# A hybrid attention block on one core: forgetting scores negated, mask and minimum in one instruction, 1/sum applied at the branch; the two halves of each head's output stored apart and added in DRAM

## The chip, the cores and the metric

The kernel runs on one core of a Trainium2 chip. The metric is the device time of one execution in microseconds. The engines are TensorE (PE, with its weight loads PEld), VectorE (DVE), ScalarE (ACT), GpSimd (POOL) and SyncE (SP); each has its own queue of instructions and works it off in order. DMAs are issued from the queues of SP and POOL.

## The reference, cut to what matters

One decoder block over 1024 positions of width 1024: three gated attention branches (8 stick-breaking heads of 64, 8 forgetting heads of 64, 4 heads of 128 over 256 memory tokens), merged, and a squared-ReLU MLP. All in float32. The change touches the two causal kinds of heads and, in two lines, the others.

```python
def stick_breaking_attention(q, k, v):
    ...
        z = einsum(q, k) * HD ** -0.5
        strict = s_idx < t_idx
        log_rem = where(strict, log_sigmoid(-z), 0.0)
        after = cumsum(log_rem, reverse=True) - log_rem
        w = where(strict, exp(log_sigmoid(z) + after), 0.0)
        outs.append(einsum(w, v))

def forgetting_attention(q, k, v, log_f):
    F = cumsum(log_f)
    ...
        z = einsum(q, k) * HD ** -0.5
        z = z + F[t] - F[s]
        p = softmax(where(s_idx <= t_idx, z, NEG_INF))
        outs.append(einsum(p, v))

def reference(...):
    h = rmsnorm(x)
    ... = split(h @ w_in)                       # q, k, v of all heads, forget logits, gate logits
    o_fox = forgetting_attention(rmsnorm(fx_q), rmsnorm(fx_k), fx_v, log_sigmoid(f_logit + b_forget))
    ...
    merged = gate0 * (o_sb @ w_branch_sb) + gate1 * (o_fox @ w_branch_fox) + gate2 * (o_mem @ w_branch_mem)
    x = x + merged @ w_out
    x = x + relu(rmsnorm(x) @ w_ff_up) ** 2 @ w_ff_down
```

## The kernel before, in words

**Numbers.** Each float32 operand of a product is split into a high and a low part that PE takes at its faster rate (`hi` and `lo`, or `h` and `l` in the tiles' names), and a product is made of three passes: hi·hi, hi·lo, lo·hi. ACT copies the high part (L1029 for weights, `whi`), DVE subtracts it from the whole (L1030, `wlo`).

**What sets the order.** The program does not issue instructions as it is read. Each piece of work is a generator that yields `Op(engine, cost, fn)`, takes buffers with `Get` from lists of free ones (`Places`) and gives them back with `put`, and waits for an `Event`. A planner plays all generators forward in time with costs by formula (`mm_time`, `act_time`, `dve_time`, `SMALL` for a 128x1 instruction) and emits each instruction when its turn comes. What comes out is one fixed order for each engine. The hardware then runs it, with semaphores between the engines. A cost changed in one place so moves instructions everywhere behind it, and an instruction that takes longer on the chip than the planner charged makes its engine late against that order.

**Stages.** To about 340 us: the norm, the projections of all heads, the turning of queries and keys. 340 to 850: attention. 830 to 1000: the three branch products, in the order memory, stick-breaking, forgetting (`bring`, L1550, gets a branch's operand). Then merge, output product and MLP. Between the instructions of attention, the planner places the products of the gates (L1119, weights loaded as `raw<-w_in` on POOL's queue at L1037), so that PE is always fed.

**Attention.** Heads go in pairs, first the four stick-breaking pairs, then the four forgetting ones. A pair loads its queries and keys (`h`, L979) and values (`v`, L1015) on POOL's queue. A unit (`unit`, L875) is one head with two query tiles of 128; a pair has eight units. A query tile's keys come in one or two chunks of up to 512 columns, each with a score bank `sc` in PSUM (two banks).

For a stick-breaking tile (`sb_tile`, L785): scores on PE (L795), on the diagonal a mask added (the tile `strict`), two sigmoids on ACT (L800), a running product on DVE (L814). For a forgetting tile (`fox_tile`, L823), chunk by chunk: scores on PE (L837, L838; the forgetting sums F ride along as four more rows of the queries and keys, from `fq_scr` and `fk_scr`), on the diagonal a mask added (L843, the tile `above`), the maximum (L844), its negative (L845), then the exponential on ACT with its row sum (L848). After both chunks: the joint maximum (L856), factors for the chunks, the reciprocal of the sum (L865, L867), and a scaled copy of the whole weight tile on ACT (L871).

Then the weights are turned on PE (L904) and split (ACT L909 `pth`, DVE L911 `ptl`), and multiplied with the values on PE (L921) into the one `pv` bank. The part from the high values stands in its rows 0 to 63 and that from the low ones in its rows 64 to 127; their sum is the output. ACT copies the one half to a tile `ob` (L939; there are three), DVE adds the other (L940), and SP stores the 64x256 result to `o_scr` (L942), from where the branch reads it (L1554).

**Tiles.** PSUM: three `pp`, two `sc`, two `tr`, one `pv`. SBUF: `h`, `v`, `e` (weight tiles), `r` (also lent elsewhere by the name RR), `raw`, `ob`. The mask `above` (128x129: zeros and, above the diagonal, -1e30) is made on POOL at the program's start.

## Time and profile before

| | before |
|---|---|
| median of three runs | 1706.46 us (1706.36 to 1706.93) |
| the profiled execution | 1706.93 us, of which the profile's span is 1705.1 |
| HBM read, written | 181.44 MB, 88.60 MB |
| PE clock granted | 1.00 |

The page of the profile gives busy times of engines over the span, the chain of waits that ended last, and groups of instructions by line. Names right of the arrow are what an instruction reads. A table by stretches has, for each stretch of time: its bounds, its length, the busy time (and number of instructions) of PE, PEld, DVE, ACT, POOL, the granted clock of PE, the mean share of DMA engines that are busy, and GB/s. A row of waits reads: engine, tile and line of the one that waits, then what it waits for, then the time in all, the number, and the longest. A row of a timeline: start, duration, engine, line, operation, tiles, and in brackets the wait ahead of it and who ended it. A row of a tile or a line: durations as shortest, median and longest in ns, and from when to when in the program.

### The profile page before, as it was taken

The numbers are of one execution on the slowest core, as the hardware profiler recorded it, in microseconds if no ns is written. First come the engines' busy times: TensorE is split into PE (matmuls) and PEld (weight loads), VectorE is DVE, ScalarE is ACT, GpSimd is POOL, SyncE is SP. The second block draws the span as 40 slices with busy tenths as digits, with TensorE's granted clock in tenths as the row PEclk, the third lists the DMA queues.
The fourth block names the chain that finished last, engine by engine and source line by source line (L and its number), as shares of the span: only waits on it lengthen the run. The fifth ranks groups of instructions, "written<-read, shape, count | busy, mean of one in ns | idle before, by whom it ended". The sixth has DMA issues, their size and how long they took to land.

```text
span 1705.1 us, 25350 instructions
## 1 busy us (share of the span) xinstructions
PE 1691.7 (99%) x9186; PEld 1442.8 (85%) x9186; DVE 1346.3 (79%) x2321; ACT 886.8 (52%) x1635; POOL 256.0 (15%) x441
## 2 busy tenths in 40 slices
PE   9999999999999999999999999999999999999998
PEld 9998899998888888888888887878888887888887
DVE  7977678868999888888656898987777776788775
ACT  6445555556676798889733446533233344332331
POOL 0000000043322233241000011021211120000000
PEclk9999999999999999999999999999999999999999
DMA  7545444576544453553375642144444484554532
GB/s 242 162 144 191 135 124 149 157 245 187 160 128 123 113 176 112 183 164 110 100 238 168 217 179 94 56 162 141 156 153 149 142 289 180 195 206 148 198 123 74
DMA packets 131406, 271.72 MB, mean 159 GB/s; under 512 B 15761, under 2 KB 43409, under 8 KB 131281
## 3 DMA queue, kind: packets, MB, share of 16 engines
q1 hardware_dynamic: 99600, 169.94, 29.2%
q0 software_dynamic: 31680, 100.17, 19.5%
q8 instruction: 72, 1.18, 0.3%
q14 instruction: 54, 0.43, 0.1%
HBM read 181.44 MB, written 88.60 MB: 158 GB/s over the span
## 4 chain that ended last, share of the span: by engine, by line
PE 83%; issue 7%; DVE 5%; DMA 2%; POOL 2%; ACT 1%; SPq 0%; POOLq 0%; DVEq 0%; ACTq 0%
PE pp L1119 21%; PE pp L2518 7%; PE pp L1405 7%; PE pp L1848 6%; PE sc L1405 5%; PE tr L904 4%; PE tr L2518 4%; PE sc L2518 4%; PE sc L1119 3%; PE sc L1848 3%; PE pv L2518 2%; PE pv L921 2%; PE pp L921 2%; PE pv L1405 2%; POOL s_scr L1865 2%
## 5 line engine op out<-in xcount | busy, mean ns | idle before, releaser
L1119 PE MATMUL pp<-hi,whi 128*128 128x512 f32 x368 | 147.6, 401 | 0.0
L1119 PE MATMUL pp<-hi,wlo 128*128 128x512 f32 x368 | 145.0, 394 | 0.0
L1119 PE MATMUL pp<-lo,whi 128*128 128x512 f32 x368 | 144.8, 393 | 0.0
L1030 DVE TENSOR_TENSOR wlo<-raw,whi 128x1024 fp32r<-128x1024 f32 (+1 forms) x82 | 100.0, 1221 | 38.9 <-ACT whi L1029 38.6
L2518 PE MATMUL pp<-h,sop 128*128 128x512 f32 x540 | 128.7, 395 | 1.4 <-DVE sop L1784 1.4
L2518 PEld LDWEIGHTS pp<-h,sop 128*128 128x128 f32 x540 | 101.1, 187 | 26.5 <-DVE sop L1784 1.8
L1848 PE MATMUL pp<-h,oh 128*128 128x512 f32 x384 | 120.9, 396 | 0.7 <-ACT cu L1934 0.6
L1029 ACT ACTIVATE whi<-raw 128x1024 fp32r<-128x1024 f32 (+1 forms) x82 | 86.8, 1059 | 52.4 <-PE pp L1405 18.7
L911 DVE TENSOR_TENSOR ptl<-tr,pth 128x512 fp32r<-128x512 f32 (+1 forms) x160 | 98.8, 627 | 11.0 <-ACT pth L909 10.6
L909 ACT ACTIVATE pth<-tr 128x512 fp32r<-128x512 f32 (+1 forms) x160 | 86.7, 558 | 28.5 <-PE tr L904 15.5
L814 DVE TENSOR_TENSOR_SCAN r<-r,sm 128x896 f32<-128x896 f32 (+4 forms) x64 | 85.5, 1345 | 3.5 <-ACT r L799 3.4
L2436 ACT ACTIVATE h<-t 128x2048 fp32r<-128x2048 f32 x16 | 30.7, 1919 | 110.4 <-DVE t L1784 97.9
L1848 PEld LDWEIGHTS pp<-h,oh 128*128 128x128 f32 x384 | 71.7, 187 | 19.2 <-ACT cu L1934 1.5
L1119 PEld LDWEIGHTS pp<-hi,wlo 128*128 128x128 f32 x368 | 69.1, 188 | 16.4
L1119 PEld LDWEIGHTS pp<-lo,whi 128*128 128x128 f32 x368 | 69.5, 189 | 10.3
L1119 PEld LDWEIGHTS pp<-hi,whi 128*128 128x128 f32 x368 | 69.4, 189 | 10.1
L1848 PE MATMUL pp<-h,ol 128*128 128x512 f32 x192 | 75.9, 396 | 0.0
L1841 ACT ACTIVATE oh<-raw 128x512 fp32r<-128x512 f32 x64 | 39.4, 625 | 61.7 <-DVE raw L1784 61.7
L2518 PE MATMUL sc<-h,sop 128*128 128x512 f32 x264 | 63.4, 395 | 0.0
L2518 PE MATMUL tr<-h,sop 128*128 128x512 f32 x264 | 63.4, 395 | 0.0
L1784 DVE TENSOR_TENSOR sop<-ur,sop 128x2048 fp32r<-128x2048 f32 x27 | 61.7, 2286 | 1.7 <-ACT sop L2447 1.7
L844 DVE TENSOR_REDUCE st<-sc 128x1 f32<-128x512 f32 (+2 forms) x96 | 53.3, 555 | 9.3 <-PE sc L838 7.1
(586 smaller groups left out, 5102.9 us busy)
## 6 DMA issues: line engine op xcount, KB each, us to landing
ur<-s_scr SPq DMA_DIRECT2D x26, 1024.0 KB
raw<-w_in POOLq DMA_DIRECT2D x42, 512.0 KB, 5.2
raw<-w_up SPq DMA_DIRECT2D x60, 256.0 KB
s_scr<-s POOLq DMA_DIRECT2D x60, 256.0 KB, 2.5
g<-w_down SPq DMA_DIRECT2D x14, 1024.0 KB
s_scr<-cu POOLq DMA_DIRECT2D x48, 256.0 KB, 2.9
gate_scr<-o SPq DMA_DIRECT2D x44, 256.0 KB
o<-gate_scr SPq DMA_DIRECT2D x32, 256.0 KB
```

The source lines that it names most:

```text
L814: nc.vector.tensor_tensor_scan(out=rev, data0=rev, data1=zero.to_broadcast([P, n]), initial=1.0, op0=ALU.mult, op1=ALU.add)
L904: nc.tensor.transpose(tr[:, jj * 256 + a * P:jj * 256 + (a + 1) * P], es[a][:, j * P:(j + 1) * P], ident)
L909: yield Op("ACT", act_time(512 - lo_c), lambda: nc.scalar.activation(ph[:, lo_c:], tr[:, lo_c:], AF.Copy))
L911: yield Op("DVE", dve_time(512 - lo_c), lambda: nc.vector.tensor_tensor(pl[:, lo_c:], tr[:, lo_c:], f32(ph[:, lo_c:]), ALU.subtract))
L921: nc.tensor.matmul(pv[0][:, c_:256], pair.v[:, j, b, :], p_[:, jj * 256 + c_:(jj + 1) * 256], start=(k == 0 and n_ == 0 and i == 0), stop= ...
L1029: yield Op("ACT", 0.03 + act_time(m), lambda: nc.scalar.activation(hi, raw, AF.Copy))
L1030: yield Op("DVE", dve_time(m), lambda: nc.vector.tensor_tensor(lo, raw, f32(hi), ALU.subtract))
L1119: nc.tensor.matmul(ps, a_, b_, start=(first and i == 0), stop=(last and i == n - 1))
L1405: nc.tensor.matmul(out_, a_, b_, start=(first and n == 0 and j == 0), stop=(last and n == 3 and j == len(todo) - 1), skip_group_check=True)
L1784: nc.vector.tensor_tensor(out_, a_, b_, op)
L1848: nc.tensor.matmul(ps, w[a_][:, k * P:(k + 1) * P], h[b_][k], start=(first and k == 0 and i == 0), stop=(last and k == 3 and i == 2), skip ...
L2518: nc.tensor.matmul(ps, a_[:, c, qs], b_[:, c, :], start=(kind in ("P1", "P2", "P7") and c == 0 and i == 0), stop=(kind in ("P2", "P4", "P3 ...
```

## The change

**Signs.** The forgetting queries' gain and the signs of the stored F are flipped, so that the bank holds the negated scores; the stick-breaking queries are negated as they are split. All masks then are +1e30 above the diagonal, in one tile `later` of 128x513, made on POOL when attention's tiles are opened, in place of `above`.

**A forgetting tile.** The chunk on the diagonal has one DVE instruction that adds the mask and gives the row's minimum (which is the negated maximum, as the exponential's bias needs it); the other chunk has a plain minimum. A second chunk waits for the first one's minimum and takes the joint one as its bias, the exponential having scale -1. With two chunks the first is then brought to the joint minimum by one product on DVE; with one chunk nothing more is done. The weights are not divided by their sum any more. The sums are kept in columns of a tile `fn`.

**1/sum.** When a pair is through, DVE takes the reciprocal of its 16 columns and SP stores them to `l_scr`, element by element (128x16x1). The forgetting branch loads them, spread over 64 partitions for each head, and multiplies its operand by them on DVE (128x1024) before the split.

**Output halves.** ACT copies all 128 rows of the `pv` bank to `ob`, which frees the bank; SP stores the two halves apart, to `o_scr` and to `low_scr`. After a pair's eighth unit, and a pause of 4 us in the plan, POOL issues a DMA that adds 128 rows of `low_scr` to `o_scr` in DRAM. The branch of the forgetting heads waits for the event `added` in place of `over`.

**Also.** In memory attention the maximum is taken with its negative in one instruction. The tiles for small statistics are fewer and smaller.

```diff
-    above = C.p.tile([P, P + 1], F32, tag="above", name="above")
-    nc.gpsimd.memset(above, 0.0)
-    nc.gpsimd.affine_select(out=above, in_=above, pattern=[[-1, P + 1]], compare_op=ALU.is_ge,
-                            fill=NEG, base=0, channel_multiplier=1)
...
+    low_scr = [dram.tile([512, S], F32, name=f"low_scr{b}", tag=f"low_scr{b}") for b in range(2)]
+    l_scr = dram.tile([8, S], F32, name="l_scr", tag="l_scr")
...
-            nc.vector.tensor_scalar(gq2, gq2, HD ** -0.5, None, ALU.mult)
+            nc.vector.tensor_scalar(gq2, gq2, -HD ** -0.5, None, ALU.mult)
...
+    def sums_kept(h0):
+
+        cols = fn[:, 8 * h0:8 * h0 + 16]
+        yield Op("DVE", SMALL, lambda: nc.vector.reciprocal(cols, cols))
+        yield Op("SP", 0.4, lambda: nc.sync.dma_start(
+            l_scr[h0:h0 + 2, :].rearrange("h (i p) -> p (h i)", p=P), cols, allow_slow_non_contiguous=True), 4.0)
...
-                nc.vector.tensor_reduce(mx, sc.rearrange("p (t m) -> p t m", m=MEM), AX.X, ALU.max)
-                nc.vector.tensor_scalar(mx, mx, -1.0, None, ALU.mult)
+                nc.vector.tensor_reduce(mx, sc.rearrange("p (t m) -> p t m", m=MEM), AX.X, ALU.max, negate=True)
...
             def maxima():
                 if c + u == n:
-                    dg = sc[:, u - P:u]
-                    nc.vector.tensor_tensor(dg, dg, tri, ALU.add)
-                nc.vector.tensor_reduce(mx[:, ci:ci + 1], sc[:, :u], AX.X, ALU.max)
-                nc.vector.tensor_scalar(nx[:, ci:ci + 1], mx[:, ci:ci + 1], -1.0, None, ALU.mult)
+                    nc.vector.tensor_tensor_reduce(sc[:, :u], sc[:, :u], holder["later"][:, 512 - u:512], 1.0, -NEG,
+                                                   ALU.add, ALU.min, nx[:, ci:ci + 1])
+                else:
+                    nc.vector.tensor_reduce(nx[:, ci:ci + 1], sc[:, :u], AX.X, ALU.min)
             yield Op("PE", mm_time(cols, cols), scores)
-            yield Op("DVE", (0.22 if c + u == n else 0.0) + dve_time(u) + SMALL, maxima)
+            yield Op("DVE", dve_time(u), maxima)
+            bias = nx[:, 0:1]
+            if ci == 0:
+                machine.fire(first_max)
+            else:
+                yield first_max
+                bias = m
+                yield Op("DVE", SMALL, lambda: nc.vector.tensor_tensor(m, nx[:, 0:1], nx[:, 1:2], ALU.min))
             yield Op("ACT", act_time(u) + 0.21, lambda: nc.scalar.activation(
-                e[:, c:c + u], sc[:, :u], AF.Exp, bias=nx[:, ci:ci + 1], accum_out=l[:, ci:ci + 1]), table=AF.Exp)
+                e[:, c:c + u], sc[:, :u], AF.Exp, scale=-1.0, bias=bias,
+                accum_out=l[:, ci:ci + 1] if two else total), table=AF.Exp)
             SC.put(sc)
...
-            yield Op("DVE", SMALL, most)
-            yield Op("ACT", 0.22, lambda: nc.scalar.activation(f, mx, AF.Exp, bias=m[:, 0:1]), table=AF.Exp)
-
-        def scale():
...
-        def scaled():
-            for ci, (c, _, u) in enumerate(ch):
-                nc.scalar.activation(e[:, c:c + u], e[:, c:c + u], AF.Copy, scale=f[:, ci:ci + 1])
-        yield Op("DVE", SMALL * (4 if two else 1), scale)
-        yield Op("ACT", act_time(*[u for _, _, u in ch]) + 0.0002 * n, scaled)
+            yield Op("ACT", 0.22, lambda: nc.scalar.activation(f, nx[:, 0:1], AF.Exp, scale=-1.0, bias=m), table=AF.Exp)
+
+            def scaled():
+                nc.vector.tensor_scalar(e[:, :512], e[:, :512], f, None, ALU.mult)
+                nc.vector.scalar_tensor_tensor(total, l[:, 0:1], f, l[:, 1:2], ALU.mult, ALU.add)
+            yield Op("DVE", dve_time(512) + SMALL, scaled)
...
         ob = yield Get(OB)
-        o = ob[:HD, :]
-        yield Op("ACT", act_time(256), lambda: nc.scalar.activation(o, pv[0][HD:P, :256], AF.Copy))
-        yield Op("DVE", dve_time(256), lambda: nc.vector.tensor_tensor(o, o, pv[0][0:HD, :256], ALU.add))
+        yield Op("ACT", act_time(256), lambda: nc.scalar.activation(ob, pv[0][:, :256], AF.Copy))
         PV.put(pv[0])
-        yield Op("SP", 0.1, lambda: nc.sync.dma_start(scr[r0:r0 + HD, g * 256:(g + 1) * 256], o), 2.5)
+        dst = scr[r0:r0 + HD, g * 256:(g + 1) * 256]
+        low = low_scr[pair.kind != "sb"][r0:r0 + HD, g * 256:(g + 1) * 256]
+
+        def halves():
+            nc.sync.dma_start(dst, ob[:HD, :])
+            nc.sync.dma_start(low, ob[HD:, :])
+        yield Op("SP", 0.2, halves, 3.0)
         OB.put(ob)
         pair.units += 1
         if pair.units == 8:
             VV.put(pair.v_)
+            if pair.kind == "fox":
+                yield from sums_kept(2 * pair.p)
             machine.fire(pair.over)
+            yield Sleep(4.0)
+            rows = slice(pair.p * P, pair.p * P + P)
+            yield Op("POOL", 0.8, lambda: nc.gpsimd.dma_start(
+                scr[rows, :], low_scr[pair.kind != "sb"][rows, :], max_dma_last_dim=2048, accum_op=ALU.add), 4.0)
+            machine.fire(pair.added)
...
+    def masked(t):
+        nc.gpsimd.memset(t, 0.0)
+        nc.gpsimd.affine_select(out=t[:, 384:], in_=t[:, 384:], pattern=[[-1, P + 1]], compare_op=ALU.is_ge,
+                                fill=-NEG, base=0, channel_multiplier=1)
...
-        yield from transfer(lambda: nc.sync.dma_start(raw[:, :S], src), P * S * 4)
+        if bi == 2:
+            sums = yield Get(RR)
+
+        def issue():
+            nc.sync.dma_start(raw[:, :S], src)
+            if bi == 2:
+                for i, half in enumerate((slice(0, HD), slice(HD, P))):
+                    nc.sync.dma_start(sums[half, :], l_scr[2 * k + i:2 * k + i + 1, :].partition_broadcast(HD))
+        yield from transfer(issue, P * S * (8 if bi == 2 else 4))
+        if bi == 2:
+            yield Op("DVE", dve_time(S), lambda: nc.vector.tensor_tensor(raw[:, :S], raw[:, :S], sums, ALU.mult))
+            RR.put(sums)
...
         for pair in pairs[4:]:
-            yield pair.over
+            yield pair.added
```

The planner's costs changed, so its order did. Three places are shown: each has the rows of one engine's queue as they stand before and, under them, now. The lines of the new kernel are some 15 further down (the pair's loads at L979 are at L992, the weights' at L1037 are at L1050).

The first place is POOL's queue early in attention, in the stick-breaking pairs. The `h` rows load a pair's queries (`sbq_scr`) and keys (`sbk_scr`), the `raw` row a gate's weights; the number behind `x` counts rows that follow each other. Before:

```order
L979 DMA h_3932<-sbq_scr_85 64x512
L979 DMA h_3932<-sbq_scr_86 64x512
L979 DMA h_4103<-sbk_scr_87 64x512 x2
L979 DMA h_4102<-sbk_scr_88 64x512 x2
L1037 DMA raw_165<-w_in 128x8x128
L979 DMA h_4106<-sbk_scr_87 64x512 x2
```

Now:

```order
L992 DMA h_3930<-sbq_scr_83 64x512
L992 DMA h_3930<-sbq_scr_84 64x512
L1050 DMA raw_163<-w_in 128x8x128
L992 DMA h_4103<-sbk_scr_85 64x512 x2
L992 DMA h_4102<-sbk_scr_86 64x512 x2
L992 DMA h_4106<-sbk_scr_85 64x512 x2
```

The weight load stood behind the loads of two key tiles (four transfers) and now stands ahead of them.

The second place is DVE's queue in a forgetting tile with two chunks. `sc` is a score bank, `st` a tile of small statistics, `e` the weights, `ptl` the low part of turned weights. Before:

```order
L844 TENSOR_REDUCE st_6508<-sc_132 128x1
L845 TENSOR_SCALAR st_6508<-st_6508 128x1
L856 TENSOR_TENSOR st_6448<-st_6448 128x1
L843 TENSOR_TENSOR sc_133<-sc_133,above 128x128
L844 TENSOR_REDUCE st_6508<-sc_133 128x1
L845 TENSOR_SCALAR st_6508<-st_6508 128x1
```

Now:

```order
L852 TENSOR_REDUCE st_6114<-sc_130 128x1
L913 TENSOR_TENSOR ptl_4090<-tr_133,pth_4088 128x384
L873 TENSOR_SCALAR e_3938<-e_3938,st_6113 128x512
L874 SCALAR_TENSOR_TENSOR fn<-st_6113 128x1
L849 ISA sc_131,st_6114<-sc_131,later_3945 128x512
L849 ISA st_6114 128x1
L861 TENSOR_TENSOR st_6114<-st_6114 128x1
```

Mask, maximum and negative of the chunk on the diagonal are the two rows of L849, and the joining of both chunks (L861) follows at once, ahead of the exponential; the rows L873 and L874 are of the tile before this one.

The third place is POOL's queue at the end of attention, ahead of the branch products. `fxq_scr` and `fq_scr` are a forgetting pair's queries and sums, `w_in` weights of gates, `w_b` those of a branch. Before:

```order
L979 DMA h_3927<-fxq_scr_89 64x512
L979 DMA h_3927<-fq_scr 4x512
L1037 DMA raw_165<-w_in 128x8x128
L1037 DMA raw_166<-w_in 128x8x128
L1037 DMA raw_165<-w_b 128x4x256
L1037 DMA raw_166<-w_b 128x4x256 x3
```

Now:

```order
L992 DMA h_4107<-fxq_scr_87 64x512
L992 DMA h_4107<-fq_scr 4x512
L1050 DMA raw_163<-w_in 128x8x128
L958 DMA o_scr_75<-low_scr_78 256x512
L1050 DMA raw_164<-w_in 128x8x128
L1050 DMA raw_163<-w_in 128x8x128
L1050 DMA raw_164<-w_in 128x8x128
L958 DMA o_scr_75<-low_scr_78 256x512
L1050 DMA raw_163<-w_b 128x4x256
L1050 DMA raw_164<-w_b 128x4x256 x2
```

Two of the adding transfers (L958) now stand among the last loads of weights.

47 lines of the change are left out of this document (23 added, 24 removed).

## The prediction

> **What bounds the kernel now.** The page is read first, for the engine that is never free:
>
> ```profile
> span 1705.1 us, 25350 instructions
> PE 1691.7 (99%) x9186; PEld 1442.8 (85%) x9186; DVE 1346.3 (79%) x2321; ACT 886.8 (52%) x1635; POOL 256.0 (15%) x441
> ...
> PE 83%; issue 7%; DVE 5%; DMA 2%; POOL 2%; ACT 1%; SPq 0%; POOLq 0%; DVEq 0%; ACTq 0%
> ```
>
> The matmul engine (PE) works 99% of the span, and the chain that ended last lies on it for 83%. An average can hide a stage with another limit, so the table by stretches comes next. The change acts on 340 to 1000 us: stick-breaking heads to about 590, forgetting heads to about 850, then the branch products.
>
> ```profile
> 350.00:400.00 50.00, 49.03 (x307) 43.36 (x306) 36.42 (x58) 30.60 (x65) 22.31 (x40) 1.00 0.76 238
> 400.00:600.00 200.00, 200.00 (x1174) 173.90 (x1173) 183.10 (x298) 140.11 (x306) 57.59 (x100) 1.00 0.48 137
> 600.00:850.00 250.00, 250.00 (x1509) 218.12 (x1508) 204.95 (x641) 211.22 (x544) 70.69 (x126) 1.00 0.46 140
> 850.00:950.00 100.00, 99.95 (x431) 80.76 (x430) 60.86 (x85) 35.97 (x52) 6.77 (x9) 1.00 0.64 211
> 950.00:1000.00 50.00, 50.00 (x216) 40.33 (x215) 44.81 (x66) 22.59 (x29) 0.00 (x0) 1.00 0.57 204
> 1000.00:1050.00 50.00, 48.34 (x218) 38.77 (x217) 48.79 (x78) 29.66 (x55) 6.14 (x5) 1.00 0.32 111
> ```
>
> Behind the length of each stretch stand the busy times of PE, weight loads, VectorE (DVE), ScalarE (ACT) and GpSimd (POOL). From 400 to 850 us PE has no idle time at all, at a granted clock of 1.00, although DVE (183 of 200) and then ACT (211 of 250) come near. Third, the waits of PE, which are the stock from which any gain must come:
>
> ```profile
> PE pp L2173 <- ACT h L2148: 1.6, 1, 1.6
> PE pv L401 <- POOL ident masks.py:199: 1.5, 1, 1.5
> PE tr L451 <- DVE xt L435: 1.4, 1, 1.4
> PE pp L2518 <- DVE sop L1784: 1.4, 1, 1.4
> PE pp L1119 <- DVE wlo L1030: 1.0, 2, 0.8
> PE sc L795 <- ACT es L800: 1.0, 1, 1.0
> ```
>
> Inside the stage that changes, one wait is named: 1.0 us before a stick-breaking score (L795). The order has 8,855 rows on PE before and after; the change neither adds nor removes a matmul. So the reasoning is short: work taken off DVE and ACT is worth nothing by itself. What counts is whether PE's one wait goes, and whether new waits come.
>
> **The one wait.** Its history, on ACT, PE and POOL's DMA queue:
>
> ```profile
> 388.12 1.06 ACT L1029 ACTIVATE whi<-raw 128x1024 fp32r<-128x1024 f32 x1 [3.04 <-DMA raw<-w_in]
> 390.33 0.50 PE L795 MATMUL sc<-h,h 128*128 128x512 f32 x1 [0.97 <-ACT es L800]
> 377.54 2.07 POOL L979 DMA_DIRECT2D h<-sbk_scr  x4
> 380.33 0.94 POOL L1037 DMA_DIRECT2D raw<-w_in  x1 [0.72 <-issue]
> ```
>
> ACT stands 3.04 us for a gate's weights that land at 388.1, the sigmoids behind it come late, and PE stands 0.97. In the new order that load is issued ahead of the four h loads, so 2.07 + 0.72 = 2.8 us earlier. If it lands as much earlier, ACT waits 0.2 us and PE's 1.0 us goes. If the DMA engines are simply full at that time, nothing is won. **Term: -1.0** (0 to -1.0); I take the full gain, since the four h loads themselves share those engines.
>
> **The mask built late.** A memset of 128x513 and a select now stand on POOL ahead of the first pair's loads. The old 128x129 pair took 212 and 295 ns; with the memset four times as long this is at most 1.2 us.
>
> ```profile
> 340.75 2.07 POOL L979 DMA_DIRECT2D h<-sbk_scr  x4 [8.61 <-PE sc L1405]
> ...
> 365.04 0.93 POOL L1015 DMA_DIRECT2D v<-v_sb  x1 [18.72 <-DMA v_sb<-sn]
> ...
> L795 PE MATMUL sc<-h,h x72: 278/390/497, 365.2 to 591.6; 128*128 128x512 f32 x36, 128*128 128x256 f32 x24, 128*128 128x384 f32 x12
> ```
>
> The loads start at 341 and the first score at 365.2: 24 us of cover. **0**; without it, 1.2.
>
> **A forgetting tile's chain.** For the chunk on the diagonal three instructions (mask, maximum, its negative) become two rows in the order, the fused one and a 128x1 row that reads its accumulator.
>
> ```profile
> L844 DVE TENSOR_REDUCE st<-sc 128x1 f32<-128x512 f32 x48 | 32.9, 686 | 7.6 <-PE sc L838 7.1
> L843 DVE TENSOR_TENSOR sc<-sc,above 128x128 f32<-128x128 f32 x64 | 18.7, 292 | 6.8 <-PE sc L838 5.7 <-ACT pth L909 0.8
> L845 DVE TENSOR_SCALAR st<-st 128x1 f32<-128x1 f32 x96 | 14.7, 154 | 3.3
> L911 DVE TENSOR_TENSOR ptl<-tr,pth 128x512 fp32r<-128x512 f32 x95 | 64.4, 680 | 5.0 <-ACT pth L909 5.0
> L814 DVE TENSOR_TENSOR_SCAN r<-r,sm 128x512 f32<-128x512 f32 x8 | 9.7, 1213 | 0.0
> L848 ACT ACTIVATION_READ_ACCUMULATOR e<-sc,st 128x1 f32 x64 | 12.8, 201 | 0.0
> L871 ACT ACTIVATE e<-e,st 128x512 f32<-128x512 f32 x64 | 37.6, 639 | 2.7 <-DVE st L865 1.8 <-DVE st L856 0.6
> L871 ACT ACTIVATE es<-es,st 128x128 f32<-128x128 f32 (+3 forms) x32 | 17.7, 561 | 0.6 <-DVE st L867 0.5
> PEld sc L837 <- ACT e L848: 0.7, 3, 0.3
> ```
>
> Before, 512 columns took 0.29 + 0.69 + 0.15 = 1.13 us. The fused instruction is not in this trace: it reads two operands and keeps a running minimum, so it costs between an elementwise one (0.68) and the scan, the one row with a running value (1.21); its read between the 128x1 rows' 0.15 and ACT's 0.20. I take 0.68 + 0.15 = 0.83, as an ordinary reduction runs at the elementwise pace (0.69). The chain is then 0.30 shorter. But the planner charged 0.22 + 0.62 + 0.19 = 1.03 for the three and charges 0.62 for the one, so it puts the next score on PE 0.41 earlier: against its place the score bank comes free 0.41 - 0.30 = 0.11 us later than now. The last row shows the reserve: of 96 score groups three now find the exponential a little late, 0.7 us together on the weight loads, nothing on PE. With 0.11 more, some six of the 64 diagonal chunks lose about 0.1 each. **Term: +0.5** (0 to the first rival's 4.8).
>
> The rest of that chain falls away or moves: ACT loses 37.6 + 17.7 = 55 us of scaling copies; two-chunk tiles get one 128x512 product on DVE; the second chunk waits for the first one's minimum, and the 0.15 us instruction that joins the two only moves ahead of the exponential. DVE and ACT both get lighter, and PE, which had no idle time, cannot take the difference: it runs the same gate products after the heads that it ran between them. **0.** Were ACT the limit, 55 us would be the prize. The sign moved into the queries' gain and the forgetting sums changes operands of instructions that exist: 0.
>
> **Output halves.**
>
> ```profile
> L940 DVE TENSOR_TENSOR ob<-ob,pv 64x256 f32<-64x256 f32 x33 | 13.4, 405 | 7.6 <-ACT ob L939 7.5
> L942 SPq DMA_DIRECT2D o_scr<-ob x64: 445/446/559, 390.1 to 845.4; - x64
> L468 SPq DMA_DIRECT2D sm<-g_mq x1: 1008/1008/1008, 24.7 to 24.7; - x1
> raw<-w_in POOLq DMA_DIRECT2D x42, 512.0 KB, 5.2
> v<-v_sb POOLq DMA_DIRECT2D x4, 1024.0 KB, 7.2
> ```
>
> 64 additions of 0.40 leave DVE, and the single pv bank comes free that much sooner. 64 more stores of 0.45 us go to SP's queue: 29 us in 455, on a queue that issues one o_scr store in 7; three ob tiles cover it: **0**, and behind that cover an ACT instruction that waits for a tile. Eight accumulating transfers of 512 KB join POOL's queue; each waits there for its pair's stores, and behind it stand loads for the next pairs and weights. Nothing in the trace accumulates. Its bytes are read twice and written once: between a 512 KB load (5.2 us to landing) and, with 2.0 us for each further 512 KB as from 5.2 to 7.2, 9.2 us. What reads the sums is the branch, over 20 us later: **0**, the second rival aside. Four stores of sums, 2,048 single elements each, join SP's queue: between 0.45 each, as a row store, and 16 times the 1.0 us in which 128 elements were issued. Every SP queue entry behind is a store with two more tiles free: **0**, the third rival aside.
>
> **The 1/sum at the branch.** Four products of 128x1024 on DVE, 1.2 us each by the split of the same shape, and 4 x 0.5 MB of reads:
>
> ```profile
> L1030 DVE TENSOR_TENSOR wlo<-raw,whi 128x1024 fp32r<-128x1024 f32 x23 | 28.0, 1216 | 1.6 <-ACT whi L1029 1.5
> L1554 SPq DMA_DIRECT2D raw<-o_scr x12: 319/320/560, 797.6 to 905.3; - x12
> L151 PE MATMUL sc<-h,whi x28: 392/394/398, 939.2 to 983.3; 128*128 128x512 f32 x28
> ```
>
> The last such load goes out at 905.3 and its branch starts near 939: 34 us for a load, 1.2 us of product and the split, while DVE is busy 61 of 100 us (850 to 950). **0**; uncovered, 4.9.
>
> **Sum.** The durations are from the profiled execution, 1706.93 us (its span of 1705.1 and 1.8 around it): 1706.93 - 1.0 + 0.5 = 1706.4. That execution was the slowest of three, 0.47 above their median of 1706.46, so I forecast **1706.0 us**: no change.
>
> **Rivals.** (1) The fused instruction runs like the scan: 1.21 + 0.20 = 1.41, 0.28 longer than the three and 0.69 late against its place. If a quarter of the 64 diagonal chunks then cost PE 0.3 us, 16 x 0.3 = 4.8: 1710.8. For it: the running value; against: the plain reduction at 0.69.
>
> (2) Slower through POOL's queue: the accumulations delay a weight load right behind them. Before the first branch products the order has two of them among the last gates' and the branches' weights. A load that now lands after 5.2 us comes 9.2 - 5.2 = 4 us later if it shares the engines with one, and PE loses what exceeds the load's lead. At 388 us a lead of nothing cost PE 1.0, so the place is tight at times; from 400 to 850, with none lost, it was not. Two times 4 us: +8, 1714.0. It decides from the point where an accumulation takes longer than the lead of one weight load. The Trainium skill (Collectives: The Full Stack, "The bandwidth ceiling: the fold count and why AG ≠ RS ≠ AR") says that a reduction in the DMA path reads two sources for each chunk and so gets about half a copy's rate; by it the accumulation would take about twice a copy's time. No run yet shows it.
>
> (3) Slower through SP's queue: at 16 us for one store of sums (16 x 1.0), the unit stores behind it wait. Units come every 455 / 64 = 7.1 us; two free ob tiles last 14, so ACT stands 2 us, four times: +8, 1714.0. It decides above 14 us. Against: rows of 128 and more elements take 0.32 to 0.56 to issue. The Trainium skill (DMA: Bandwidth & Descriptors, "Rules for kernel authors") says that a non-contiguous last dimension becomes one descriptor per element and should be rearranged, which speaks against this store; no row here has 2,048 of them.
>
> (4) Faster: the lighter DVE also removes the waits at L1119 (1.0) and L2173 (1.6), with the 1.0 of L795: 1706.46 - 3.6 = 1702.9. Against: DVE is idle 39 of 100 us from 850 to 950, so no backlog reaches 1000.
>
> **How the numbers follow.** Forecast 0.63, rivals 0.12, 0.13, 0.07 and 0.05. I count 0.2%, 3.4 us, as what a measurement can tell from no change: 1703.1 to 1709.9. Inside fall the forecast and about 0.08 of the rivals in milder form (a third of the first, a sixth of the others): same 0.71. Slower 0.25, faster 0.04. The range goes from 1704.8 (the 1.0, and half of the 1.0 at L1119) to 1712.0, past the first rival; it leaves out the last, and most of the second and third.
>
> **What would show it.** After: PE waits between 350 and 1000 us of about 1 us in all, at places with scores (L837's successor), none of 1.0 near 390; ACT busy in the forgetting heads down by some 55 us; the fused row near 0.68 for 512 columns. Wrong it would be if PE had idle time of several us between 400 and 950, with the accumulation, a weight load or the sums' store as its releaser.

## The result, and the profile after

| | before | changed |
|---|---|---|
| median on record (20 executions each) | 1706.99 us | 1711.16 us (1705.02 to 1715.43) |
| ratio to before | | 1.0020, interval 1.0011 to 1.0029 |
| the profiled execution, its span | 1706.93, 1705.1 us | 1713.1, 1711.3 us |
| the changed kernel again, three later sets (11 executions each) | | 1705.21, 1706.12, 1706.89 us |
| their ratios to before | | 0.9995, 0.9995, 1.0003 (each 0.9986 to 1.0004 or 0.9995 to 1.0012) |

On record the change made the kernel 0.2% slower; in three later sets on other runs of the same two kernels nothing could be measured. The kernel before stayed between 1706.2 and 1707.0 in all sets. (The ratios are those on record, with their intervals; they are not quotients of the medians and differ from these by up to 0.1%.) So two things have to be explained: what the changed kernel lost in the profiled execution, and why that loss comes and goes.

The page of the changed kernel, its span, busy times, chain and DMA packets:

```profile
span 1711.3 us, 25187 instructions
PE 1692.4 (99%) x9186; PEld 1445.0 (84%) x9186; DVE 1293.3 (76%) x2057; ACT 832.7 (49%) x1539; POOL 266.4 (16%) x449
...
DMA packets 147596, 282.23 MB, mean 165 GB/s; under 512 B 25296, under 2 KB 57040, under 8 KB 147472
...
PE 72%; issue 10%; DVE 6%; DMA 4%; POOL 2%; ACT 1%; SPq 0%; POOLq 0%; DVEq 0%; ACTq 0%
```

DVE lost 53 us of work and ACT 54; PE's work is what it was (1692.4 against 1691.7), and the span grew by 6.2. On the chain of waits, PE's share fell from 83 to 72%, and "issue" and DMA took most of it. So PE stood idle more, and the list of its waits says where:

```profile
PE sc L798 <- ACT e L803: 3.4, 1, 3.4
PE pp L2207 <- ACT h L2182: 2.6, 1, 2.6
PE sc L844 <- ACT e L862: 2.5, 1, 2.5
PE pv L398 <- POOL ident masks.py:199: 1.4, 1, 1.4
PE pp L1132 <- DVE wlo L1043: 1.1, 2, 0.9
PE tr L448 <- DVE xt L432: 1.1, 2, 0.6
PE sc L2125 <- DVE raw L1818: 1.0, 1, 1.0
PE pp L2552 <- DVE sop L1818: 0.9, 1, 0.9
PE pp L1882 <- ACT cu L1968: 0.6, 1, 0.6
PE pp L1132 <- DVE lo L457: 0.2, 1, 0.2
```

These come to 14.8 us. Before, the list came to 8.7 (the six rows of the prediction, and two of 0.6 and 0.2). The difference is 6.1, close to the 6.2 of the span, though a lower clock behind one of the waits also cost time (below), so the agreement is not exact bookkeeping. Three waits are new or longer: **379 us** (a stick-breaking score, L798), **725 us** (a forgetting score, L844) and **the merge** (L2125 and L2207, 3.6 where L2173 had 1.6). The table by stretches shows the same three:

```profile
350.00:400.00 50.00, 46.58 (x279) 41.06 (x278) 30.88 (x48) 25.10 (x54) 22.15 (x40) 0.97 0.75 235
400.00:600.00 200.00, 200.00 (x1192) 174.24 (x1191) 179.94 (x273) 141.58 (x320) 59.61 (x103) 1.00 0.55 153
600.00:850.00 250.00, 247.50 (x1496) 216.53 (x1495) 158.44 (x408) 161.53 (x445) 76.53 (x132) 1.00 0.67 156
850.00:950.00 100.00, 100.00 (x433) 80.89 (x432) 59.18 (x82) 33.17 (x49) 6.77 (x9) 1.00 0.70 211
...
1000.00:1050.00 50.00, 46.37 (x204) 37.13 (x203) 49.41 (x77) 24.99 (x46) 8.43 (x4) 1.00 0.28 95
```

In the forgetting heads (600 to 850) DVE and ACT are now far from full (158 and 162 of 250 in place of 205 and 211), and yet PE, which had no idle time there, stands 2.5 us. The DMA share went from 0.46 to 0.67 while the bytes rose only from 140 to 156 GB/s: the DMA engines are busy longer for each byte.

**379 us.** The timeline of POOL's queue, ACT and PE there:

```profile
365.10 0.92 POOL L1028 DMA_DIRECT2D v<-v_sb  x1 [18.74 <-DMA v_sb<-sn]
366.00 0.90 POOL L1050 DMA_DIRECT2D raw<-w_in  x1
366.88 3.13 POOL L992 DMA_DIRECT2D h<-sbk_scr  x6
374.79 0.52 POOL L992 DMA_DIRECT2D h<-sbk_scr  x1 [4.77 <-DMA v<-v_sb]
...
371.49 0.61 ACT L803 ACTIVATE e<-sc 128x512 f32<-128x512 f32 x1
376.65 1.06 ACT L1042 ACTIVATE whi<-raw 128x1024 fp32r<-128x1024 f32 x1 [4.55 <-DMA raw<-w_in]
377.61 0.58 ACT L802 ACTIVATE r<-sc 128x512 f32<-128x512 f32 x1
...
378.73 0.52 PE L798 MATMUL sc<-h,h 128*128 128x256 f32 x1 [3.42 <-ACT e L803]
379.26 0.63 PE L1132 MATMUL pp<-hi,whi 128*128 128x512 f32 x1
379.69 0.63 PE L1132 MATMUL pp<-lo,whi 128*128 128x512 f32 x1
```

A gate's weights go out at 366.0, right behind v, and land at 376.6. ACT has their split next in its queue and stands 4.55 us; the sigmoids behind it, which would free the score banks, come late, and PE stands 3.42. In the kernel before, the same load went out at the same time (365.96), but ACT did four more sigmoids ahead of that split and stood 0.77 us, which no score noticed. So it is ACT's order that changed here, at an instruction that none of the edits touches.

**725 us.** The wait at L844 has the same form. ACT has the split of another gate's weights ahead of an exponential, and that load went out at 706.7 and landed only after 15.5 us:

```profile
722.28 1.06 ACT L1042 ACTIVATE whi<-raw 128x1024 fp32r<-128x1024 f32 x1 [3.20 <-DMA raw<-w_in]
```

**A forgetting tile.** Groups of DVE by form in the changed kernel, 560 to 860 us:

```profile
L849 DVE CUSTOM_DVE_ANT_0 sc<-sc,later 128x512 f32<-128x512 f32 x16 | 11.1, 695 | 4.1 <-PE sc L845 4.1
L849 DVE DVE_READ_ACCUMULATOR2_ANT st<- 128x1 f32 x64 | 9.1, 142 | 0.0
```

The fused instruction runs at the pace of a plain reduction (0.69 before), and with the read of its accumulator it takes 0.695 + 0.142 = 0.84 us.

### The profile page after: what moved, and what is told of

Its sections match the earlier page's. It is cut to its first block, busy times and chain, and to the rows that moved or that the text cites. A ratio compares the mean times of both kernels' runs of the same rounds, so it can differ in the third digit from the quotient of the medians.

```text
span 1711.3 us, 25187 instructions
## 1 busy us (share of the span) xinstructions
PE 1692.4 (99%) x9186; PEld 1445.0 (84%) x9186; DVE 1293.3 (76%) x2057; ACT 832.7 (49%) x1539; POOL 266.4 (16%) x449
## 4 chain that ended last, share of the span: by engine, by line
PE 72%; issue 10%; DVE 6%; DMA 4%; POOL 2%; ACT 1%; SPq 0%; POOLq 0%; DVEq 0%; ACTq 0%
PE pp L1132 17%; PE pp L2552 7%; PE pp L1418 7%; PE sc L1418 5%; PE pp L1882 4%; PE tr L2552 4%; PE sc L2552 4%; PE tr L906 4%; PE pv L2552 2%; POOL s_scr L1899 2%; PE pv L923 2%; PE pp L923 2%; PE pv L1418 2%; PE sc L1132 2%; PE sc L1882 2%
## 5 line engine op out<-in xcount | busy, mean ns | idle before, releaser
L1132 PE MATMUL pp<-hi,whi 128*128 128x512 f32 x352 | 141.4, 402 | 0.0
L1132 PE MATMUL pp<-hi,wlo 128*128 128x512 f32 x352 | 139.4, 396 | 0.0
L1132 PE MATMUL pp<-lo,whi 128*128 128x512 f32 x352 | 138.8, 394 | 0.0
L818 DVE TENSOR_TENSOR_SCAN r<-r,sm 128x896 f32<-128x896 f32 (+5 forms) x64 | 85.4, 1349 | 9.1 <-ACT r L802 9.1
L1875 ACT ACTIVATE oh<-raw 128x512 fp32r<-128x512 f32 x64 | 39.4, 625 | 61.8 <-DVE raw L1818 61.8
L802 ACT ACTIVATE r<-sc 128x512 f32<-128x512 f32 (+3 forms) x96 | 47.9, 499 | 29.4 <-DVE sc L808 18.3
```

The lines of the kernel that those rows point to most:

```text
L818: nc.vector.tensor_tensor_scan(out=rev, data0=rev, data1=zero.to_broadcast([P, n]), initial=1.0, op0=ALU.mult, op1=ALU.add)
L1132: nc.tensor.matmul(ps, a_, b_, start=(first and i == 0), stop=(last and i == n - 1))
```

## The experiments

Names: **P** is the theory that the plan's order made the wait at 379, **R** that the single-element stores of the sums (128x16x1, 2,048 elements a pair) delay the loads issued behind them, **Q** that the accumulating DMAs do. Ratios are to the kernel before in the same set.

### First set: the mask's planned cost, the accumulations, the stores of sums

**The mask without a planned cost.**

```diff
-        yield Op("POOL", 1.0, lambda: masked(later))
+        masked(later)
```

> The changed kernel, with the mask made without a planned cost (the two POOL instructions are issued at the same place, but the planner charges nothing for them). Theory P (the plan): the 1.0 us that the planner charges on POOL moves the split of a gate's weights on ACT ahead of four sigmoids, in front of a load that lands too late; PE then stands 3.4 us near 379 us and runs some 3 us at a lower clock after it. Then in this kernel the split stands behind the four sigmoids again, the wait of PE at the second row of sigmoids is 1 us or less, and the time falls by 3 to 5 us against the changed kernel, to about 1706 to 1708 (ratio to before 0.9995 to 1.0006), if the rest of the plan, which moves too, brings no new wait. Rival (the accumulating transfers and the other new operations are the whole cost): the wait near 379 may go, but the time stays at 1.002 of before.

1715.28 us, ratio 1.0048 (1.0036 to 1.0060). The split stood behind the four sigmoids again and the wait at 379 was gone, as P says. The time was a miss: the moved plan met a wait of 7.8 us at L844 near 732 us, and the kernel was slower in all.

**The pause in the kernel before.**

```diff
+        yield Op("POOL", 1.0, lambda: None)
```

> The kernel before, with an empty planned instruction of 1.0 us on POOL where attention's tiles are opened; nothing is issued for it, no other line is changed. Theory P: ACT gets the weight split ahead of four sigmoids as in the changed kernel; PE stands 2 to 4 us near 379 us, where it now stands 0; the time rises by 2 to 5 us to about 1709 to 1712 (ratio 1.001 to 1.003), less what the plan wins or loses elsewhere. Rival (the changed operations are the cost, the plan's order is harmless): ratio within 0.0005 of 1.

1710.12 us, ratio 1.0014 (1.0005 to 1.0023). ACT's order at 372 us became that of the changed kernel, with nothing issued for it, and PE stood 1.5 us at L795 in its profile (2 to 4 were expected). One planned microsecond alone made the old kernel slower by 0.14%, so the plan's order alone can cost time, as P says. The profile shows little of that cost: it is of one of five executions that had a granted clock of 1.000 and took 1706.5 to 1707.8 us. The other seven had 0.997 to 0.999 and took 1709.7 to 1712.4; where PE stood in those is not shown.

**No accumulations**, same order:

```diff
-                scr[rows, :], low_scr[pair.kind != "sb"][rows, :], max_dma_last_dim=2048, accum_op=ALU.add), 4.0)
+                spare[at:at + 1, :], mem[at:at + 1, :]), 4.0)
```

> The changed kernel, its order unchanged, with each accumulating DMA replaced by a small one (4 KB of an input to a spare tile) at the same place of POOL's queue, that waits for no store; the low halves of the outputs are so left out of the result. Theory Q (the accumulations hold POOL's queue and the DMA engines in the forgetting stage): the wait of PE at L844 near 725 us (2.5 us) goes, the weight load there is issued 2 us or more earlier; the time falls by 2.5 to 3.5 us to a ratio of about 1.0005; the wait near 379 stays at 3 to 4. Theory R (the element-wise store of the sums is what fills the engines there): the wait at L844 stays above 1.5 us, the ratio at 1.002.

This leaves the low halves out of the result. 1708.71 us, ratio 1.0013 (1.0003 to 1.0023). The wait at L844 shrank to 0.2 us, as Q expected, but a wait of 1.6 us for a branch's weights came up, and the ratio hardly differs from that on record. On the theory R alone the wait should have stayed above 1.5: the weight load of 702.2 us still landed only after 13.3 us, but the next one, whose split the score waits for, went out at 712.9 us, against 715.1 in a later profile of the changed kernel. So the accumulations have a share in that one wait; that they cost the kernel time is not shown.

**Sums in rows of 8**, same order:

```diff
-            l_scr[h0:h0 + 2, :].rearrange("h (i p) -> p (h i)", p=P), cols, allow_slow_non_contiguous=True), 4.0)
+            l_scr[h0:h0 + 2, :].rearrange("h (p i) -> p h i", p=P), cols.rearrange("p (h i) -> p h i", h=2)), 4.0)
```

> The changed kernel, its order unchanged, with the 2,048 sums of a pair stored in runs of 8 elements (256 runs) in place of single elements; the sums so stand at other places than the branch expects, so the forgetting heads' scaling is left wrong in the output. Theory R: the DMA share around 650, 704, 770 and 825 us falls from 0.67 towards 0.5 (600 to 850 us), accumulations behind the stores land in 6 to 8 us in place of 13 to 18, the wait at L844 near 725 us (2.5 us) falls below 1, and the time by 2 to 3 us to a ratio of about 1.0008. Theory Q: the accumulations stay at 13 to 18 us, the wait stays, the ratio at 1.002.

The sums so stand at other places than the branch reads. 1703.36 us, ratio 0.9982 (0.9974 to 0.9991): faster than the kernel before, and all eleven executions had a granted clock of 1.000. The DMA row of its page, its stretch from 600 to 850, and the longest of PE's waits:

```profile
DMA packets 140428, 282.23 MB, mean 166 GB/s; under 512 B 18128, under 2 KB 49872, under 8 KB 140304
```

```profile
600.00:850.00 250.00, 250.00 (x1499) 218.77 (x1498) 157.25 (x402) 159.94 (x441) 76.37 (x132) 1.00 0.56 161
```

```profile
PE sc L798 <- ACT e L803: 1.7, 1, 1.7
PE pv L398 <- POOL ident masks.py:199: 1.4, 1, 1.4
PE pp L1132 <- DVE wlo L1043: 1.1, 2, 0.9
PE pp L2552 <- DVE sop L1818: 0.9, 1, 0.9
```

7,168 small packets are gone (four stores of 2,048 elements became 256 runs each), PE has no idle time from 600 to 850, and the wait at L844 and the merge's are away.

### Second set: is it the elements?

**Rows of 8, read in that order at the branch**, so that nothing is left out:

```diff
-            yield Op("DVE", dve_time(S), lambda: nc.vector.tensor_tensor(raw[:, :S], raw[:, :S], sums, ALU.mult))
+            yield Op("DVE", dve_time(S), lambda t=raw[:, :S].rearrange("c (i p) -> c i p", p=P): nc.vector.tensor_tensor(t, t, sums.rearrange("c (p i) -> c i p", p=P), ALU.mult))
```

> The changed kernel, its order unchanged, with a pair's sums stored in runs of 8 elements and the product at the branch reading them in that order (DVE with a step of 8 elements), so that nothing is left out. Theory R (the stores of single elements are the cost, not where the sums land): the time of the run with rows, 1702 to 1705, ratio 0.9975 to 0.999; the strided product takes 1.2 us as the plain one, or up to 2.4, which the branch hides. Rival (the run with rows was faster because of what it left wrong): 1.001 or more.

1709.07 us, ratio 1.0019 (1.0010 to 1.0027): a miss. The wait at L844 stayed away, but the product with a step of 8 elements takes nearly twice the time. The line of the product (shortest, median and longest in ns), in the kernel with rows:

```profile
L1587 DVE TENSOR_TENSOR raw<-raw,r x4: 1217/1226/1226, 891.0 to 924.8; 128x1024 f32<-128x1024 f32 x4
```

The same line in this one, and two of PE's waits, both in the merge:

```profile
L1587 DVE TENSOR_TENSOR raw<-raw,r x4: 2207/2231/2243, 892.1 to 927.6; 128x1024 f32<-128x1024 f32 x4
```

```profile
PE pp L2207 <- ACT h L2182: 3.6, 1, 3.6
...
PE sc L2125 <- DVE raw L1818: 1.2, 1, 1.2
```

4 x 1.0 us more on DVE, in a stretch where it is busy 59 of 100 us, go with 4.8 us of waits in the merge, 70 to 120 us later; the two other kernels with this product have 5.3 and 5.0 there. What "covered" meant there had to be looked at (next section).

**Elements in the kernel before**: one store of 128x16 single elements, read by nobody, behind each forgetting pair's last output store, same order:

```diff
+            if pair.kind == "fox" and pair.stored == 8:
+                nc.sync.dma_start(spare[2 * pair.p:2 * pair.p + 2, :].rearrange("h (i p) -> p (h i)", p=P), ident[:, :16],
+                                  allow_slow_non_contiguous=True)
```

> The kernel before, its order unchanged, with one extra store at the end of each forgetting pair: 128x16 single elements to a spare tile that nobody reads, behind the pair's last output store on SP's queue. Theory R: loads issued in the 15 us behind each of these stores land after 10 to 15 us in place of 5 to 9, and where a weight load is among them PE stands; the time rises by 3 to 8 us, ratio 1.002 to 1.005, with single waits of PE of 2 us or more behind 640, 695, 760 or 815 us. Rival (the stores cost only because the accumulations share the time, or only the changed order is sensitive): ratio below 1.001, no such wait.

1717.34 us, ratio 1.0065 (1.0052 to 1.0078): four stores of 8 KB cost the old kernel 11 us, more than was expected. The longest wait is at the branch, where an operand's load stood behind the last of them; the stretches, and the timeline of SP's queue, ACT and PE there:

```profile
600.00:850.00 250.00, 247.97 (x1496) 214.94 (x1495) 206.34 (x646) 212.21 (x547) 70.36 (x126) 1.00 0.56 139
850.00:950.00 100.00, 95.28 (x399) 76.45 (x398) 52.06 (x75) 30.87 (x46) 6.74 (x9) 0.97 0.58 181
```

```profile
850.63 0.58 SPq L948 DMA_DIRECT2D spare<-ident  x1
...
867.37 1.15 ACT L1037 ACTIVATE h<-raw 128x512 fp32r<-128x512 f32 x2 [9.81 <-DMA raw<-o_scr]
...
869.51 0.50 PE L1127 MATMUL pp<-h,whi 128*128 128x512 f32 x1 [3.68 <-ACT whi L1037]
```

From 600 to 850 PE, which had no idle time there before, stands 2.0 us, and from 850 to 950 it stands 4.7 us. R holds, without any other part of the change. The store itself takes 0.58 us to issue: SP's queue is not what it blocks.

**Rows, and the mask unplanned**: the two edits together.

> As the first of this set, and the mask made without a planned cost. Theory P: the wait of PE at the second row of sigmoids (1.7 us with rows, 3.4 in the changed kernel) goes, as it did in the first run of the mask; theory R: the wait of 7.8 us that stood at L844 near 732 in that run goes too; the time is 1700 to 1703, 1 to 3 us under the first of this set. Rival: the plan as a whole was worse there (1715), and stays above 1706.

1707.58 us, ratio 1.0009 (1.0001 to 1.0018). Both waits were gone, at 379 and at L844 (the 7.8 us of the first mask run too), as P and R say. The time missed the 1700 to 1703 us that were expected: the waits in the merge that go with the strided product (2.7 and 2.7) kept it up.

**Rows, no accumulations**: likewise.

> As the first of this set, its order unchanged, with the accumulating DMAs replaced by small ones, so that the low halves of the outputs are left out. If the accumulations cost nothing once the stores of sums are in rows (theory R alone): within 0.7 us of the first of this set. Theory Q (they cost time of their own): 1 to 3 us faster than it.

1711.99 us, ratio 1.0044 (1.0031 to 1.0058), slower than with the accumulations. Its weight load of 365.5 us landed after 11.7 us, and PE stood 4.5 us near 379. Q is not borne out: nothing was won by taking the accumulations away. That R alone holds is not shown by this run either, since it is not within 0.7 us of the first of the set.

### Third set: sums turned on PE, and the changed kernel again

```diff
-        yield Op("DVE", SMALL, lambda: nc.vector.reciprocal(cols, cols))
+        tr, ob = (yield Get(TR)), (yield Get(OB))
+        yield Op("PE", 0.06, lambda: nc.tensor.transpose(tr[:16, :P], cols, ident))
+        yield Op("DVE", SMALL, lambda: nc.vector.reciprocal(ob[:16, :P], tr[:16, :P]))
+        TR.put(tr)
...
+            l_scr[h0:h0 + 2, :].rearrange("h (i p) -> (h i) p", p=P), ob[:16, :P]), 2.5)
```

> The changed kernel with a pair's 16 columns of sums turned on PE (one 128x16 instruction), their reciprocals written by DVE as 16 rows of 128, and stored as rows of 512 bytes; the product at the branch reads them with step 1; nothing is left out. The plan moves a little behind the first forgetting pair. Theory R (the single elements are the cost) with the stride's cost known from the strided run: the merge's waits at L2125 and L2207 are under 1 us together, no load behind a store of sums lands after more than 10 us, and the time is 1702 to 1705, ratio 0.9975 to 0.999. Rival (the kernel with rows was fast for another reason): 1.001 or more.

1706.21 us, ratio 0.9996 (0.9987 to 1.0005): no wait at L844, 0.8 us at 379, 1.7 in the merge; not the 0.9975 to 0.999 that R expected, and no different from the changed kernel beside it.

> As the first of this set, and the mask made without a planned cost. Theory P: the wait at the second row of sigmoids (1.0 to 4.5 us in all runs with the planned microsecond) is absent; with R the time is 1700 to 1703, ratio 0.9965 to 0.998. Rival: what the plan wins there it loses at another place, and the two of this set agree within 1 us.

1704.19 us, ratio 0.9989 (0.9978 to 0.9999). Neither wait is in its profile; it is the fastest that leaves nothing out in this set, at the lower edge of what can be told from no change. The 1700 to 1703 us that P and R together expected were missed.

> The changed kernel itself. Theory P (the wait near 379 us is as long as the weight load issued at 366 us lands late, and its landing varies between executions, 8.4 to 11.7 us so far): the wait lies between 1 and 4.5 us and is 6 to 8 us shorter than the landing takes; times spread over 1705 to 1715 as before, ratio 1.002 to 1.003. Rival (a fixed delay in the order): 3.4 us again whatever the landing.

1705.21 us, ratio 0.9995. The load of 365.9 us landed after 8.7 us and PE stood 1.4 us at 379; at L844 it stood 1.9; the merge's new waits were absent.

> The kernel of the run with rows of 8 sums, its order unchanged, without the loads of the sums and the product at the forgetting branch (the 1/sum is left out of the result). If the 1/sum at the branch is covered: within 0.7 us of that run, 1703 to 1704, ratio near 0.998. If the branch has no cover for it (theory S, to which the strided product points, where 4 us more on DVE made the merge wait 8): 2 to 4 us faster, ratio 0.996 to 0.997.

1704.07 us, ratio 0.9987 (0.9978 to 0.9997). The loads of the sums and the product cost nothing that can be told: in both kernels with rows the merge has next to no wait.

### Fourth and fifth set: each on one chip

The next four share one chip. The swap puts the first gate weight load of attention ahead of the first load of v on POOL's queue, everything else as in the changed kernel:

> The changed kernel itself, beside the next three on one chip. By P and R: times in two groups some 4 us apart (the weight load's landing at 8.7 or at 10.6 us and more), 1703 to 1706 and 1707 to 1712, the share of the groups differing from chip to chip; the wait at L844 of 1.9 to 2.5 us in each.

> The kernel of the run with rows of 8 sums, again, its order that of the changed kernel (the sums so stand at other places than the branch expects, which leaves the scaling wrong). By R: 2 to 3 us faster than the changed kernel on the same chip (the wait at L844), in two groups some 4 us apart like it. Rival (the first result with rows was the chip's): the same as the changed kernel within 1 us.

> The changed kernel, its order unchanged but for two neighbours on POOL's queue: the first gate weight load of attention is issued ahead of the first load of v, which waits 18.7 us for its stores, in place of behind it. By P: the load lands more than 5 us before its split, PE's wait near 379 is gone in every execution, the time falls by 1.4 us against the faster group of the changed kernel and by 4 to 5 against its slower group, and the spread of the runs narrows. Rival (the load waits for its tile, not for the queue): it goes out no earlier, and nothing changes.

> The kernel that turns the sums on PE, with the same swap. By P and R together: no wait near 379 and none at L844 over 1 us; 3 to 5 us faster than the changed kernel on this chip, ratio to before 0.997 to 0.9985. Rival: 0.9995 or more.

| kernel | median | ratio | wait at 379 | wait at L844 |
|---|---|---|---|---|
| changed | 1706.12 | 0.9995 (0.9986 to 1.0004) | 1.1 | 1.0 |
| rows of 8 | 1703.69 | 0.9989 (0.9978 to 0.9999) | 1.5 | none |
| weights first | 1702.91 | 0.9979 (0.9970 to 0.9988) | none | 1.1 |
| turned, weights first | 1703.74 | 0.9993 (0.9981 to 1.0005) | none | none |

Each wait goes with its cause. The swapped load goes out 20 us earlier, since it no longer stands behind v:

```profile
345.67 0.92 POOL L1053 DMA_DIRECT2D raw<-w_in  x1
364.39 0.89 POOL L1030 DMA_DIRECT2D v<-v_sb  x1 [17.80 <-DMA v_sb<-sn]
```

By their medians the rows are worth 2.4 us and the swap 3.2, but both intervals overlap that of the changed kernel, the swap's barely. Turned sums and swap together did not add up. The last set put the swap beside the changed kernel on another chip:

> The changed kernel, beside the next. Between 1705 and 1711.5 us by the chip it falls on; by P its slower executions are 3 to 5 us above its faster ones.

> The changed kernel with the first gate weight load ahead of the first load of v, again. By P: 1702 to 1704, ratio to before 0.997 to 0.999, 3 us or more under the changed kernel beside it, more where that one is slow. Rival (the slow executions are late in another place): it moves with the changed kernel and is 1 to 2 us under it.

1706.89 us (1.0003) and 1705.96 us (1.0001, 0.9989 to 1.0014). The wait at 379 was again away, but the profiled execution of the swapped kernel stood 2.8 us in the merge and 1.7 at L844. So the swap's gain did not come again, and no version that leaves nothing out was faster than both kernels in more than one set.

## Why the prediction was right or wrong

The forecast was 1706.0 us, no change. The three later sets agree with it, the set on record does not: it moved, by +0.2%, to 1711.16 (inside the range). That the later sets come within 1 us is in part luck, since in their profiles old waits went (L795's 1.0 and more than half of L2173's 1.6 us) and new ones of 2.1 to 3.3 us in all came at 379 and L844. The prediction's own sign of being wrong, PE idle for several us between 400 and 950 behind a weight load, came as 2.5 us at 725; the larger wait, 3.4 us at 379, lies outside that stretch. By its own steps:

**"The one wait. Term: -1.0."** The wait at 390 us did go, but not as the step had it. The load was not out 2.8 us earlier: in the profiled execution it went out at 380.46 (before: 380.33), since POOL's queue stood 4.77 and 1.60 us ahead of it. It landed at 386.8 in place of 388.1, and ACT stood 0.22 us for it. Moreover the step looked at POOL's order alone. On ACT, the split of the load before that one had moved ahead of four sigmoids, and what stood there was a wait of 1 to 4.5 us. How long depends on when that load lands, and this differs between executions:

| execution (all with this order on ACT) | load of 366 us lands after | PE waits at L798 |
|---|---|---|
| no accumulations | 8.4 us | 1.0 us |
| changed, third set | 8.7 | 1.4 |
| rows of 8 | 9.1 | 1.7 |
| changed, on record | 10.6 | 3.4 |
| rows, no scale | 11.7 | 4.5 |

The wait is the landing less 7.2 to 7.4 us, here and in the other profiles of this order, but for the kernel with turned sums (8.7 and 0.8). This is the term that failed first: -1.0 was forecast, +2.4 net came in the profiled execution, and some 1.5 us more went into a lower clock behind it (0.97 granted over 50 us). In the three later profiles, 1.1 to 1.4 us stood in place of the 1.0. In the kernel before, that load lands as late (after 8.7 us in its profile, 10.4 in the kernel with elements), but four sigmoids stand between it and PE, which stood 0 and 0.4 us.

**"The mask built late. 0."** The two instructions on POOL are covered: they ran at 309 us and took 0.55 and 0.29. What cost time is the 1.0 us that the planner charges for them: it moved the sigmoids in the plan and so the split ahead of them. The pause in the kernel before and the mask without a planned cost show it from both sides.

**"A forgetting tile's chain. +0.5."** The forecast was 0.83 us for the fused pair; 0.84 was measured. The first rival (1.41) falls. The +0.5 us that the step put on it is not seen: the profiles with the sums in rows have no wait at a forgetting tile's score (L844).

**"DVE and ACT both get lighter, and PE ... cannot take the difference. 0."** This was right: DVE has 53 us less work and ACT 54, and PE gained nothing by it. (PE has 9186 instructions in both pages; the prediction's 8,855 rows are in no view.)

**"Output halves."** In the profile on record the accumulations landed after 5.7 to 6.5 us in the stick-breaking heads, inside the 5.2 to 9.2 given, and after 13.2 to 18.5 behind the element stores. With the sums in rows and the same order it was up to 9.6. (Where the mask is unplanned one at 605 us took 11.9 to 13.6 without an element store; why is not shown.) The second rival's mechanism, an accumulation that delays the weights by 4 us twice, did not show: taking them away won nothing that could be told. The Trainium skill (Collectives: The Full Stack, "The bandwidth ceiling: the fold count and why AG ≠ RS ≠ AR") would have made them about twice a copy's time, an estimate from the half rate that it states; against a 512 KB load's 5.2 us, those of 5.7 to 6.5 took 1.1 to 1.3 times it, and here the measurement decides.

**"Four stores of sums ... 0, the third rival aside."** Here the mechanism was wrong and so the price. The store was feared for SP's queue; it takes 0.38 us to issue. What it holds up are transfers of other queues too: a gate's weight load that POOL issued 2.3 us behind one landed after 14.1 us. The changed kernel of the fourth set:

```profile
L1050 POOL DMA_DIRECT2D raw<-w_in x1: 937/937/937, 703.2 to 703.2; - x1
...
DMA to landing us min/median/max: 14.1/14.1/14.1
```

The kernel with rows beside it:

```profile
L1050 POOL DMA_DIRECT2D raw<-w_in x1: 936/936/936, 703.4 to 703.4; - x1
...
DMA to landing us min/median/max: 7.7/7.7/7.7
```

The DMA engines' busy share from 600 to 850 us says the same: 0.67 with elements (on record) and 0.56 with rows (first set), at 156 and 161 GB/s. The price is 1.0 to 2.5 us at L844 in all six profiles of the changed order with elements and accumulations, and none with rows or turned sums; in the kernel before it was 11 us. The Trainium skill says both halves of it (DMA: Bandwidth & Descriptors, "Rules for kernel authors"): single elements become a descriptor each, and queues of different engines share the same DMA engines. The prediction cited the first and drew only SP's queue from it; the runs agree with both (7,168 packets fewer with rows, and the two landings above).

**"The 1/sum at the branch. 0."** This was right, but the cover behind it is thin, and the plan's order takes most of it. The cover is DVE's idle time between 905 and 965 us. SP's queue now has two loads of a branch's weights (`w_b`) ahead of the merge's gates (`gt`), where it had one, and the second stands for the first. Before:

```profile
935.79 0.38 SPq L140 DMA_DIRECT2D raw<-w_b  x1
936.27 3.47 SPq L1753 DMA_DIRECT2D gt<-gate_scr  x2
```

Now:

```profile
939.87 9.40 SPq L137 DMA_DIRECT2D raw<-w_b  x2
949.33 0.97 SPq L1787 DMA_DIRECT2D gt<-gate_scr  x2
```

So the gates come late, and DVE starts the merge later than it did, waiting 4 us for them:

```profile
954.93 0.69 DVE L1818 TENSOR_TENSOR tmp<-sc,gt 128x512 f32<-128x512 f32 x1 [4.33 <-ACT gt L1793]
...
975.98 0.69 DVE L1818 TENSOR_TENSOR tmp<-pp,gt 128x512 f32<-128x512 f32 x1 [1.86 <-ACT gt L1793]
```

Before, DVE began at 943.5. Here it is 11.5 us later, while PE, place for place in its order, is 4.8 us late. In the three later profiles it is 4.9 to 5.5 us later, and PE within 0.5 us of its old place: some 5 us of the cover are used up. The 1/sum is not what uses them: measured against PE's place, DVE starts the merge 4.6 us late in the first kernel with rows, and 4.7 in the one without the sums' loads and the product. From there DVE is all but full until 1040 (39.3 and 39.4 of 40 us, from 960 and from 1000 us, in the changed kernel of the fourth set; on record 37.6, with the second wait above, and 40.0), so what it is late beyond some 5 us, PE waits for at L2125 and L2207 (6.7 us late against PE on record, with 3.6 us of waits; 5.4 and 5.5 in the fourth and fifth set, with 0.6 and 0.5). The second wait above, 1.9 us, came in the execution on record and not in the three others. The first kernel with the strided product is 7.7 us late by this count, with 5.3 us of waits.

**The fourth rival** (faster, 1702.9: the lighter DVE takes the waits at L1119 and L2173 away) had 0.05. The kernels with rows came to 1703.4 and 1703.7, and the wait of 1.6 us at L2173 (L2207 now) was gone in the first and 1.0 in the second; that at L1119 stayed. These two have the sums at other places than the branch reads; of the kernels that turn their sums and leave nothing out, the first shows no gain (0.9996). So a gain of the change itself without the elements is not shown. (The range's lower end is 0.2 off its own terms: 1706.46 - 1.5 is 1705.0, not 1704.8; nothing hangs on it.)

**Left open** is why the set on record was some 5 us above the later ones as a whole. Part of it is the clock: 18 of its 20 executions have a granted clock below 1.000, with a mean of 0.9984, against 4 to 7 of 11 and means of 0.9993 to 0.9996 in the later sets. A clock lower by 0.0009 to 0.0013 over some 1706 us costs at most 1.6 to 2.2 us (an estimate from these means). The waits at 379, at L844 and in the merge were each at their longest in its profile, among the profiles of this order with elements and accumulations, and all three go back to a transfer that came late; what makes transfers land late together in one set is not shown. The accumulations' share of the wait at L844 is not settled either: without them and with the elements it was 0.2 us.

## What to carry to other kernels

Where a planner's costs set the order, an edit's planned cost is part of the edit: compare the queues of every engine that waits for loads, not only the one that the edit touches, and look for a load whose consumer has moved ahead of other work. Store small results in rows: a store of a few thousand single elements was charged here to the loads issued behind it on other queues too, not to its own queue alone. Where waits end at transfers, one execution shows one size of them; run the same kernel in several sets before a difference of 0.2% is believed.

## What the runs showed of the hardware

- After PE stood 3.42 us its matmuls of 512 columns began 0.43 us apart (379.26, 379.69) in place of 0.23, for some 3 us, at a granted clock of 0.50 from 378.8 to 382.2 us (0.97 over 350 to 400): a stall of 3.4 us cost about 4.9. The Trainium skill (TensorE: Matmul & The Clock Gate, "Part 1") has the array at half its clock until it has been busy some 3.4 us; the trace agrees (3.41 us). The length of one stall does not decide here: one of 1.7 us (L844, weights first, last set) had such a stretch behind it, and one of 2.6 (L2207, changed, on record) had none.
- A product of 128x1024 on DVE with one operand at a step of 8 elements of 4 bytes took 2.23 us in place of 1.23.
- POOL's queue had eight DMAs out and held the ninth until the first had landed: v, the weights and six loads of h from 365.10 on, then the next at 374.79, which waited 4.77 us for v. Whether the limit is the queue's or the program's is not shown.
